# The output projection of a decoder block as seven block products instead of eight

## The chip, the cores and the metric

One core of a Trainium2 chip. The metric is the device time of one execution in microseconds, the median of several runs. Engines are named as the profile does: PE (TensorE, matmul), DVE (VectorE), ACT (ScalarE), POOL (GpSimd) and SP (SyncE, which here only issues transfers). An instruction of one engine runs in the order of that engine's queue. A DMA is issued by an engine, and waits in its queue for whatever its issue waits for.

## The reference

One layer of a decoder trunk over 1024 tokens of width 1024, fp32. The mixers (four HGRN2 heads, four heads of dilated windows, an RWKV-7 group) give 1024 columns, which go through the output projection `w_out` and are added to x. A gated MLP and a gated input embedding follow.

```
z = rmsnorm(h, norm_mix_g) @ w_in
... # o_a: HGRN2 (512 columns), o_b: dilated windows (256), o_c: RWKV-7 (256)
h = h + concatenate([o_a, o_b, o_c]) @ w_out
h = h + conv_glu_ffn(rmsnorm(h, norm_ffn_g), ffn_up, conv_w, conv_b, ffn_down)
gate = sigmoid(rmsnorm(h, norm_ple_g) @ ple_gate)
h = h + gate * (p @ ple_proj)
return rmsnorm(h, final_norm_g)
```

## The kernel before

Everything is held transposed: eight tiles of 128 channels by 1024 tokens, the tokens in two halves of 512 (`HT`). An fp32 product is made of three: each operand is split into a high part (`hi`, a cast on ACT to the type that PE multiplies) and a low part (`lo`, what the cast lost), and high x high, high x low and low x high are summed (`mm3`, L137). Weights are split in `split2` (L110): `hi` by ACT, `lo` either by DVE or POOL as a subtraction, or, where the source in DRAM is passed, as a negation on ACT (L117) and a DMA from POOL's queue that adds the weight on to it (L118). `hi` and `lo` rotate through six buffers each (`WB`), the raw weights through two (`wraw`, L104).

The output projection is `phase_out` (L1239). `rows(m, halves)` takes the weights of one block of 128 output channels, does `dense` over the eight input tiles in the order in which the mixers finish them, and adds the result to `h`, which holds x (eight loads on ACT's queue, L1246); each half row goes to DRAM (`hd`). Row blocks 0 and 1 take both halves at once, then six left halves follow, then six right halves. The mixers' results are split by `o_split` (L1232), `lo` of the right half on POOL.

For the norm of the MLP the squares of `h` are summed into `acc` (`sq_acc`, L213: a square on ACT, an addition on DVE), four matmuls sum over the channels (`rstd`, L188), DVE and POOL make the factor (L191, L195), and four matmuls spread it over a tile (`rstd_spread`, L201). For the left half this happens between the row blocks of the right half; `ffn_norm(0, ...)` then scales and splits the left half of `h` (L1361, L1362, L1369). `pe_load` (L1319) loads two tiles of the per-layer input and two of its projection into two buffers of their own (`praw`), and splits them (`peh`, `pel`); `embed` (L1301) multiplies them after the last row block, and PE fills with its products the time until the right half's factor.

While the RWKV heads run, `project_rest` (L430) goes on with the input projection, and yields after each k-step of six products, so that its work interleaves with that of RWKV. There POOL makes `gnr` (L768), a power on which the group norm of an RWKV head waits, and issues some of the adding DMAs of `split2`. The scheduler of the tile framework sets the order of each queue; `issue_after` places a group of instructions behind another one.

## Time and profile before

| | |
|---|---|
| median of 3 runs | 1404.28 us (1402.86 to 1405.35) |
| the profiled execution | 1403.29 us, span 1401.5 us |
| granted clock of PE | 0.996 |
| PE busy | 1373.6 us, 98% of the span |
| DVE, ACT, POOL busy | 1042.6, 644.2, 361.7 us |

The profile comes from one execution; positions in it are microseconds from the start of its span. The output projection takes about 563 to 643 us of it, the embedding products and the MLP follow. A row of groups has the line, the engine, the operation, what it writes and reads, its shape, and how often; then its busy time, the mean ns of one, and how long the engine stood idle before such instructions, with what ended the idle time. A matmul's duration is longer than its share of the engine's time, since matmuls overlap.

### The profile page before, as it was taken

The numbers are of one execution on the slowest core, as the hardware profiler recorded it, in microseconds if no ns is written. First come the engines' busy times: TensorE is split into PE (matmuls) and PEld (weight loads), VectorE is DVE, ScalarE is ACT, GpSimd is POOL, SyncE is SP. The second block draws the span as 40 slices with busy tenths as digits, with TensorE's granted clock in tenths as the row PEclk, the third lists the DMA queues.
The fourth block names the chain that finished last, engine by engine and source line by source line (L and its number), as shares of the span: only waits on it lengthen the run. The fifth ranks groups of instructions, "written<-read, shape, count | busy, mean of one in ns | idle before, by whom it ended". The sixth has DMA issues, their size and how long they took to land.

```text
span 1401.5 us, 22421 instructions
## 1 busy us (share of the span) xinstructions
PE 1373.6 (98%) x8646; PEld 1114.8 (80%) x8646; DVE 1042.6 (74%) x1614; ACT 644.2 (46%) x1107; POOL 361.7 (26%) x286
## 2 busy tenths in 40 slices
PE   9999999999999999999999999999999999999997
PEld 6878777877878767788788888888888888888886
DVE  7595456835667795458889888888888799778675
ACT  7523323133355584365544343444344444455662
POOL 4210011101222232111345455445453000002231
PEclk9999999999999999999999999999999999999998
DMA  6344322533723322873232322232324963442674
GB/s 231 90 119 101 91 69 68 133 72 88 244 91 106 99 69 89 267 224 130 97 128 98 113 102 88 101 109 98 113 98 163 354 211 113 120 150 62 174 196 149
DMA packets 88475, 182.83 MB, mean 130 GB/s; under 512 B 20912, under 2 KB 23216, under 8 KB 88368
## 3 DMA queue, kind: packets, MB, share of 16 engines
q1 hardware_dynamic: 66784, 147.05, 31.0%
q0 software_dynamic: 9360, 18.88, 7.3%
q10 hardware_dynamic: 12224, 15.47, 3.2%
q8 instruction: 68, 1.11, 0.3%
q14 instruction: 39, 0.32, 0.1%
HBM read 134.96 MB, written 46.40 MB: 129 GB/s over the span
## 4 chain that ended last, share of the span: by engine, by line
PE 83%; issue 7%; DVE 5%; ACT 2%; POOL 2%; DMA 1%; SPq 0%; POOLq 0%; DVEq 0%; ACTq 0%
PE bg L1343 17%; PE bv L1343 13%; PE bv L1644 7%; PE bg L1644 7%; PE dp L142 6%; PE dp L146 6%; PE dp L144 6%; PE swq L1174 1%; PE bv L142 1%; PE bv L146 1%; PE bv L144 1%; PE hsc L1020 1%; PE zp L142 1%; PE bg L142 1%; PE bg L146 1%
## 5 line engine op out<-in xcount | busy, mean ns | idle before, releaser
L142 PE MATMUL dp<-xh,whi 128*128 128x512 f32 x544 | 187.1, 406 | 2.5 <-ACT xh L413 1.2
L144 PE MATMUL dp<-xl,whi 128*128 128x512 f32 x544 | 180.3, 393 | 0.6 <-DVE xl L414 0.5
L146 PE MATMUL dp<-xh,wlo 128*128 128x512 f32 x544 | 179.6, 392 | 0.5 <-DMA wlo<-in_w_out_dram 0.5
L120 POOL TENSOR_TENSOR wlo<-raw,whi 128x512 fp32r<-128x512 f32 x84 | 134.8, 1623 | 75.7 <-ACT whi L114 75.7
L114 ACT CAST whi<-wraw 128x512 fp32r<-128x512 f32 x120 | 72.9, 617 | 153.5 <-PE dp L144 115.4
L1343 PE MATMUL bg<-t,whi 128*128 128x512 f32 x352 | 133.4, 389 | 0.0
L144 PEld LDWEIGHTS dp<-xl,whi 128*128 128x128 f32 x544 | 102.3, 188 | 24.7 <-DVE xl L414 2.6
L146 PEld LDWEIGHTS dp<-xh,wlo 128*128 128x128 f32 x544 | 102.1, 188 | 24.7 <-issue 2.0
L142 PEld LDWEIGHTS dp<-xh,whi 128*128 128x128 f32 x544 | 98.9, 189 | 27.3 <-issue 5.9
L120 POOL TENSOR_TENSOR wlo<-s,whi 128x512 fp32r<-128x512 f32 x44 | 64.6, 1467 | 166.9 <-ACT whi L114 153.7
L1644 PE MATMUL bg<-t,whi 128*128 128x512 f32 x308 | 95.2, 390 | 0.0
L114 ACT CAST whi<-raw 128x512 fp32r<-128x512 f32 x88 | 52.5, 619 | 92.7 <-issue 48.6
L1644 PE MATMUL bv<-t,whi 128*128 128x512 f32 x308 | 94.8, 389 | 0.0
L114 ACT CAST whi<-s 128x512 fp32r<-128x512 f32 x66 | 38.9, 620 | 119.5 <-PE bg L1343 112.8
L1343 PEld LDWEIGHTS bg<-t,whi 128*128 128x128 f32 x352 | 66.0, 188 | 13.7
L118 POOL DMA_DIRECT2D wlo<-in_w_in_dram x28 | 24.8, 898 | 190.0 <-ACT wlo L117 161.6
L195 POOL TENSOR_TENSOR rst<-rst,mhalf 128x4 f32<-128x4 f32 (+1 forms) x9 | 10.1, 1127 | 233.7 <-DVE rst L191 218.0
L1640 ACT CAST t<-t 128x512 fp32r<-128x512 f32 x77 | 47.8, 622 | 45.4 <-PE bv L1644 31.1
L1343 PE MATMUL bg<-t,wlo 128*128 128x512 f32 x176 | 67.5, 389 | 0.0
L1644 PEld LDWEIGHTS bv<-t,whi 128*128 128x128 f32 x308 | 57.8, 188 | 12.0
L1644 PEld LDWEIGHTS bg<-t,whi 128*128 128x128 f32 x308 | 57.8, 188 | 11.9
L120 DVE TENSOR_TENSOR wlo<-wraw,whi 128x512 fp32r<-128x512 f32 x60 | 44.8, 751 | 29.4 <-ACT whi L114 16.5
(423 smaller groups left out, 3464.8 us busy)
## 6 DMA issues: line engine op xcount, KB each, us to landing
raw<-in_ffn_up_dram SPq DMA_DIRECT2D x44, 512.0 KB, 3.3
wraw<-in_w_in_dram SPq DMA_DIRECT2D x28, 512.0 KB, 3.8
z<-zst SPq DMA_DIRECT2D x18, 512.0 KB, 3.2
gb<-ct SPq DMA_DIRECT2D x33, 256.0 KB, 2.1
t<-gb SPq DMA_DIRECT2D x33, 256.0 KB, 2.8
t<-gt SPq DMA_DIRECT2D x33, 256.0 KB, 2.7
zl<-z SPq DMA_DIRECT2D x16, 512.0 KB, 4.6
wraw<-in_ple_gate_dram SPq DMA_DIRECT2D x16, 512.0 KB, 3.8
```

The lines of the kernel that those rows point to most:

```text
L114: self.cast = nc.scalar.copy(hi, src).ins
L118: nc.gpsimd.dma_start(lo, eng, accum_op=ALU.add)
L120: eng.tensor_tensor(lo, src, hi.bitcast(F32), ALU.subtract)
L142: nc.tensor.matmul(ps[hf], wh, xh[hf], start=first, stop=False)
L144: nc.tensor.matmul(ps[hf], wh, xl[hf], start=False, stop=False)
L146: self.step = nc.tensor.matmul(ps[hf], wl, xh[hf], start=False, stop=last).ins
L195: nc.gpsimd.tensor_tensor(r2, r, self.mhalf[:, :n], ALU.pow)
L1020: nc.tensor.matmul(sc[g:g + 64, c, :], ks[:, c * P + g:c * P + g + 64], x, start=True, stop=True)
L1174: m = nc.tensor.matmul(pq[h][:, b:b + w], d["q"][hs, qb * P:nk], d["k"][hs, b:b + w], start=True, stop=True)
L1343: nc.tensor.matmul(ps, w[part == 2][:, s], X[k][part == 1], start=start and k == part == 0, stop=k == 3 and part == 2, skip_group_check=no ...
L1640: nc.scalar.copy(xh, x)
L1644: nc.tensor.matmul(ps[m], wt[part == 2][:, m * P:(m + 1) * P], (xh, xl)[part == 1], start=k == part == 0, stop=k == NK - 1 and part == 2)
```

## The change

The 1024 x 1024 weight is taken as 2 x 2 blocks of 512 (input tiles 6, 7, 0, 1 and 4, 2, 3, 5; output blocks 0 to 3 and 4 to 7), the mixers' result as 2 x 2 blocks of four input tiles by one half of the tokens. Of these, seven block products are made instead of eight, in the order p1, p5, p3, p6, p7, p2, p4, each with four row blocks of 12 products (`job`, `mul`). Four of them need sums of weight blocks, four need sums of the mixers' tiles.

- The weight sums are made while RWKV runs (`out_sums`): in `project_rest`, at k-steps 1, 3 and 6, one step of loading, negating on ACT, adding by DMA from POOL's queue, or storing to DRAM. Over the four row blocks these are 12 negations, 20 adding DMAs, 8 loads and 16 stores, each of 128x512.
- The sums of the mixers' tiles are made where a tile is finished (`o_done`) and between the products (`turn4`, adding DMAs); each operand is split by `pair` on ACT and DVE. What is split first is held in the tiles of an operand that is done.
- The result of p1 is copied to `h` by ACT and that of p5 by DVE (`empty`), and x is added behind each by a DMA from POOL's queue; for the other two quarters x is loaded by SP (`load`). Products that belong to several quarters stay in their PSUM banks and go on being summed there.
- `behind` records an ordering (not a wait) of the instructions issued in it behind a given product: each step of `out_sums` and each of the `extra` steps that `at` puts behind a job.
- `pe_load` takes a buffer of `wraw` instead of `praw`'s own; its four loads come behind jobs 17 to 20. The left half's factor (`factor`) comes behind job 20 (the first row of p2), its spread behind job 21.
- `xpool` is divided, so that part of it is given back later; the columns of `w_out` are put in the order of the tiles on the host.

```diff
+    def behind(self, ins):
+        traced = self.nc.cur_bb.bb.instructions
+        last = traced[-1]
+        yield
+        start = next(k for k in reversed(range(len(traced))) if traced[k] is last) + 1
+        for i in traced[start:]:
+            self.tc.add_manual_dep(i, ins.name, mybir.DependencyInfo(mybir.DependencyClass.NoSync, mybir.DependencyReason.DATA))
...
+        self.sums = self.out_sums()
...
+    def out_sums(self):
+        nc, wo = self.nc, self.a["w_out"]
+        self.S = [{n: self.zpool.tile([P, HT], F32, tag=f"ws{n}{i}", name=f"ws{n}{i}") for n in "1234"} for i in range(4)]
+        for _ in range(15):
+            yield
+        for i in range(4):
+            a11, a12, a21, a22 = (wo[m][:, c] for m in (i, 4 + i) for c in (slice(0, HT), slice(HT, T)))
+            t, u = (self.spool.tile([P, HT], F32, tag="sqt", name=self.nm("wsum"), bufs=2) for _ in (0, 1))
+            def turn(x):
+                nc.scalar.activation(x, x, AF.Copy, scale=-1.0)
+            def add(x, src):
+                nc.gpsimd.dma_start(x, src, accum_op=ALU.add)
+            nc.sync.dma_start(t, a21)
+            nc.sync.dma_start(u, a22)
+            yield
+            turn(t)
+            add(u, a21)
+            yield
+            nc.sync.dma_start(self.S[i]["1"], u)
+            add(t, a11)
+            yield
+            nc.sync.dma_start(self.S[i]["3"], t)
+            turn(u)
+            yield
+            turn(t)
+            add(u, a11)
+            yield
+            add(t, a22)
+            add(u, a12)
+            yield
+            nc.sync.dma_start(self.S[i]["2"], t)
+            nc.sync.dma_start(self.S[i]["4"], u)
...
+                if k in (1, 3, 6):
+                    with self.behind(self.step):
+                        next(self.sums, None)
...
+    def pair(self, dst, src, eng=None):
+        nc = self.nc
+        hi, lo = dst
+        nc.scalar.copy(hi, src)
+        (eng or nc.vector).tensor_tensor(lo, src, hi.bitcast(F32), ALU.subtract)
+    def o_done(self, k):
+        nc = self.nc
+        if self.A is None:
             self.done.append(k)
             return
-        for hf in (0, 1):
-            self.split_x(self.O[k], hf, self.o[k][:, hf * HT:(hf + 1) * HT], alt=hf)
+        o = [self.o[k][:, HT:], self.o[k][:, :HT]]
+        if k in self.FIRST:
+            i = self.FIRST.index(k)
+            t1, t3 = self.Eo[i]
+            nc.vector.tensor_tensor(t1, o[1], o[0], ALU.subtract)
+            self.pair(self.A[i], o[0])
+            self.pair(self.B[i], t1)
+            nc.scalar.activation(t1, t1, AF.Copy, scale=-1.0)
+            nc.scalar.activation(t3, o[1], AF.Copy, scale=-1.0)
+            return
+        i = self.LAST.index(k)
+        for c in (0, 1):
+            if (k, c) not in self.parts:
+                nc.scalar.copy(self.final(k, c, None), o[c])
+        for t in self.Eo[i][::-1]:
+            nc.gpsimd.dma_start(t, self.parts[k, 1], accum_op=ALU.add)
...
+        hold = []
+        def weight(n, i):
+            if not hold:
+                t = self.wpool.tile([P, T], F32, tag="wraw", name=self.nm("wraw"), bufs=2)
+                hold.extend((t[:, left], t[:, right]))
+            t, d = hold.pop(0), src[n](i)
+            nc.sync.dma_start(t, d)
+            return self.split2(t, V if (n, i) in jobs[:16] else d)
...
+        plan = {"p1": (A, "a", 0, 1), "p5": (B, "b", 4, 0), "p3": (D, "b", 0, 0), "p6": (A, "a", 0, 0),
+                "p7": (B, "a", 4, 0), "p2": (C, "c", 0, 1), "p4": (A, "a", 4, 1)}
+        jobs = [(n, i) for n in plan for i in range(4)]
...
+        def sums(m, late):
+            self.sq_acc(acc, self.h[m][:, right if late else left], m == 0)
+        def job(n, i):
+            X, g, row, late = plan[n]
+            if i not in banks[g]:
+                banks[g][i] = self.mxp.tile([P, HT], F32, tag="mx", name=self.nm("zo"))
+            ps, start = banks[g][i], n in ("p1", "p5", "p2")
+            with ExitStack() as order:
+                if self.ends:
+                    order.enter_context(self.tc.issue_after(self.ends[-1]))
+                self.mul((ps, ws.pop((n, i)), X, start))
+            self.ends.append(self.step)
+            if n not in ("p1", "p5"):
+                gather(n, i)
+        def place(n, i):
+            X, g, row, late = plan[n]
+            return self.h[row + i][:, right if late else left], self.a["xT"][row + i][:, right if late else left]
+        def empty(n, i):
+            u, x = place(n, i)
+            if n == "p5":
+                V.tensor_copy(u, banks["b"][i])
+            else:
+                nc.scalar.copy(u, banks["a"][i])
+            nc.gpsimd.dma_start(u, x, accum_op=ALU.add)
+        def load(n, i):
+            nc.sync.dma_start(*place(n, i))
+        def gather(n, i):
+            X, g, row, late = plan[n]
+            m = row + i
+            u = place(n, i)[0]
+            V.tensor_tensor(u, u, banks[g][i], ALU.add)
+            if n in ("p6", "p7", "p2", "p4"):
+                nc.scalar.dma_start(self.hd[m][late], u)
+                if n in ("p6", "p7"):
+                    sums(m, late)
...
+        at(4, [lambda i=i: empty("p5", i) for i in range(4)])
+        at(5, [lambda i=i: (empty("p1", i), load("p3", i)) for i in range(4)])
+        at(16, [lambda i=i: load("p4", i) for i in range(4)])
+        at(3, [lambda i=i: self.pair(D[i], Lo[i][1]) for i in range(4)])
+        at(7, [lambda i=i: self.pair(A[i], Eo[i][0]) for i in range(4)])
+        at(10, [lambda i=i: self.pair(C[i], Lo[i][0]) for i in range(4)])
+        at(11, [lambda i=i: self.pair(B[i], Eo[i][1]) for i in range(4)])
+        at(12, [lambda i=i: turn4(i) for i in range(4)])
+        at(17, [lambda i=i: self.pair(A[i], Lo[i][0]) for i in range(4)])
...
+        at(16, [pools, *(lambda a=a: self.pe_load(*a()) for a in
+                         (lambda: (px, self.pxp, "pT", 0), lambda: (pw, self.pwp, "ple_proj", 0),
+                          lambda: (px, self.pxp, "pT", 1), lambda: (pw, self.pwp, "ple_proj", 1)))])
+        at(20, [factor, norm])
+        at(22, [lambda: [next(self.norm0, None) for _ in (0, 1)] for _ in range(6)])
+        for n, (p, i) in enumerate(jobs):
+            for q in range(0 if n == 0 else n + 4, min(n + 5, len(jobs))):
+                ws[jobs[q]] = weight(*jobs[q])
+            job(p, i)
+            with self.behind(self.ends[-1]):
+                for go in extra.get(n, ()):
+                    go()
...
+        ps, pb = small()
+        with self.behind(self.ends[15]):
+            self.ffn_first()
...
-    def pe_load(self, raws, dst, pool, src, k):
-        raw = raws.tile([P, T], F32, tag="praw", name=self.nm("praw"), bufs=2)
+    def pe_load(self, dst, pool, src, k):
+        raw = self.wpool.tile([P, T], F32, tag="wraw", name=self.nm("praw"), bufs=2)
         self.nc.sync.dma_start(raw, self.a[src][k])
```

Three places where the queues change. First, SP's queue in the second half of the projection. `praw` are the loads of `pe_load`, `wraw` those of the weights (in the change of one half row block each, two to a buffer), `h` the loads of x. Before:

```order
L105 DMA wraw_6300<-in_w_out_dram 128x1024
L105 DMA wraw_6348<-in_w_out_dram 128x1024
L1321 DMA praw_6437<-in_pT_dram 128x1024
L105 DMA wraw_6418<-in_w_out_dram 128x1024
L1321 DMA praw_6445<-in_ple_proj_dram 128x1024
L1321 DMA praw_6497<-in_pT_dram 128x1024
L105 DMA wraw_6478<-in_w_out_dram 128x1024
L1321 DMA praw_6538<-in_ple_proj_dram 128x1024
```

After; `wraw_6518` holds the weights of jobs 24 and 25, the first of p4, `wraw_6585` those of 26 and 27:

```order
L1479 DMA praw_6441<-in_pT_dram 128x1024
L1342 DMA wraw_6449<-in_w_out_dram 128x512
L1381 DMA h_5937<-in_xT_dram 128x512
L1342 DMA wraw_6449<-in_w_out_dram 128x512
L1381 DMA h_5938<-in_xT_dram 128x512
L1479 DMA praw_6476<-in_ple_proj_dram 128x1024
L1479 DMA praw_6510<-in_pT_dram 128x1024
L1342 DMA wraw_6518<-in_w_out_dram 128x512 x2
L1479 DMA praw_6542<-in_ple_proj_dram 128x1024
L1342 DMA wraw_6585<-in_w_out_dram 128x512 x2
```

The `praw` loads stood in buffers of their own; now they and the weights of p4 take turns in the same two, so that a load waits for the splitting of what is two buffers ahead of it.

Second, DVE's queue where the left half's `acc` is finished; `dp`, `zo` are PSUM banks, `rst` the first step of the factor. Before, where `rst_6319` is that of the left half:

```order
L1263 TENSOR_TENSOR h_5848<-h_5848,dp_6193 128x512
L221 TENSOR_TENSOR acc<-acc,sqt_6231 128x512
L1263 TENSOR_TENSOR h_5849<-h_5849,dp_6234 128x512
L120 TENSOR_TENSOR wlo_6309<-wraw_6300,whi_6307 128x512
L221 TENSOR_TENSOR acc<-acc,sqt_6272 128x512
L1325 TENSOR_TENSOR pel_6440<-praw_6437,peh_6439 128x512 x2
L1263 TENSOR_TENSOR h_5844<-h_5844,dp_6275 128x512
L191 TENSOR_SCALAR rst_6319<-ps_ss_6313 128x4
```

After; `h_5931<-h_5931,zo_6525` gathers job 20, and the sum with `sqt_6504` is the last of `acc`:

```order
L1297 TENSOR_TENSOR xl_5383<-xh_5406,xh_5382 128x512
L233 TENSOR_TENSOR acc<-acc,sqt_6435 128x512
L1387 TENSOR_TENSOR h_5937<-h_5937,dp_5973 128x512
L1297 TENSOR_TENSOR xl_5385<-xh_5408,xh_5384 128x512
L1483 TENSOR_TENSOR pel_6444<-praw_6441,peh_6443 128x512 x2
L1387 TENSOR_TENSOR h_5938<-h_5938,dp_5973 128x512
L233 TENSOR_TENSOR acc<-acc,sqt_6470 128x512
L1387 TENSOR_TENSOR h_5931<-h_5931,zo_6525 128x512
L233 TENSOR_TENSOR acc<-acc,sqt_6504 128x512
L1297 TENSOR_TENSOR xl_5387<-xh_5410,xh_5386 128x512
L203 TENSOR_SCALAR rst_6556<-ps_ss_6550 128x4
L1483 TENSOR_TENSOR pel_6479<-praw_6476,peh_6478 128x512 x2
```

The last sum now stands behind the gathering of the job behind which PE's matmul for the factor is queued; on PE, 12 products of job 21 lie between that matmul and the spread. Before, the gathering of the row behind the sums stood between the last sum and `rst` too, but behind the sum.

Third, POOL's queue near the end of the RWKV stage. Before:

```order
L768 TENSOR_TENSOR gnr_1940<-gnv_1937,mhalf 128x8
L698 MEMSET Uc_2524 128x1024
L768 TENSOR_TENSOR gnr_2052<-gnv_2049,mhalf 128x8
L118 DMA wlo_2274<-in_w_in_dram 128x512
L118 DMA wlo_2310<-in_w_in_dram 128x512
```

After:

```order
L821 TENSOR_TENSOR gnr_1973<-gnv_1970,mhalf 128x8
L751 MEMSET Uc_2569 128x1024
L455 DMA wsum_2017<-in_w_out_dram 128x512
L128 DMA wlo_2315<-in_w_in_dram 128x512
L821 TENSOR_TENSOR gnr_2093<-gnv_2090,mhalf 128x8
L128 DMA wlo_2353<-in_w_in_dram 128x512
```

The adding DMA of a `wlo`, which followed the second `gnr`, now stands ahead of it, with one of the weight sums'.

144 lines of the change are left out of this document (71 added, 73 removed).

## The prediction

> **What bounds the kernel now.** I read the page first: the busy shares and the chain that ended last.
>
> ```profile
> PE 1373.6 (98%) x8646; PEld 1114.8 (80%) x8646; DVE 1042.6 (74%) x1614; ACT 644.2 (46%) x1107; POOL 361.7 (26%) x286
> ...
> PE 83%; issue 7%; DVE 5%; ACT 2%; POOL 2%; DMA 1%; SPq 0%; POOLq 0%; DVEq 0%; ACTq 0%
> ```
>
> TensorE has work 98% of the time and stands in 83% of the chain. So a matmul that goes is worth its full cadence, and the question is only what TensorE waits for in its place. The cadence comes from the chain of waits in order of time, around the stage of the output projection (columns: start, length, what).
>
> ```profile
> 577.15 5.36 DMA wlo<-in_w_out_dram
> 582.55 0.50 PE dp L146
> ...
> 666.41 5.44 PE bg L1343 x24
> ```
>
> 24 products of 128x512 take 5.44 us, 0.227 us each (a single one lasts 0.39 us, but they overlap). The first row says that an accumulating transfer's time to landing counts from the start of its issue: issued at 577.15, landed 5.36 us later, and the matmul starts at once. The waits of TensorE between 500 and 690 us, the tail of the mixers and the projection, say what can be had there beside the matmuls:
>
> ```profile
> PE vt L1108 <- DVE ho L1102: 3.0, 2, 1.8
> ...
> PE dp L146 <- DMA wlo<-in_w_out_dram: 0.5, 1, 0.5
> ...
> PE dp L142 <- DVE h L1263: 0.4, 1, 0.4
> ```
>
> The projection itself (563 to 660 us) waits 0.9 us in all. The other engines, by stretches of 40 us (PE, PEld, DVE, ACT, POOL, then clock, DMA share, GB/s):
>
> ```profile
> 560.00:600.00 40.00, 38.96 (x172) 31.31 (x173) 16.14 (x24) 15.05 (x26) 6.50 (x7) 1.00 0.84 258
> 600.00:640.00 40.00, 40.00 (x184) 33.23 (x183) 28.27 (x46) 24.34 (x44) 5.43 (x6) 1.00 0.67 190
> 640.00:680.00 40.00, 40.00 (x184) 33.13 (x183) 35.15 (x55) 23.77 (x37) 5.55 (x5) 1.00 0.41 158
> ```
>
> VectorE is 40% busy where the projection begins, 71% in its second half, 88% behind it. What the change adds lands on an engine that has room early and none late.
>
> **What goes.** Before, 8 row blocks x 2 halves x 8 k x 3 parts = 384 products; after, 7 block products x 4 rows x 4 k x 3 parts = 336. 48 x 0.227 = **10.9 us**. The two waits of the projection (0.5 and 0.4) hang on tiles that no longer exist in that form: **0.9 us**, taken as gone. Together -11.8.
>
> **What comes.** The prices of the small operations, from the groups of 563 to 690 us (count, busy, mean ns, idle before):
>
> ```profile
> L1263 DVE TENSOR_TENSOR h<-h,dp 128x512 f32<-128x512 f32 x16 | 10.8, 684 | 22.4 <-PE dp L146 22.4
> L221 DVE TENSOR_TENSOR acc<-acc,sqt 128x512 f32<-128x512 f32 x14 | 9.6, 687 | 2.5 <-ACT sqt L220 2.3
> ...
> L120 DVE TENSOR_TENSOR wlo<-wraw,whi 128x512 fp32r<-128x512 f32 x11 | 7.6, 689 | 5.9 <-PE dp L144 4.3 <-ACT whi L114 1.6
> L117 ACT ACTIVATE wlo<-whi 128x512 fp32r<-128x512 f32 x11 | 6.9, 631 | 4.5 <-DVE h L1263 4.2
> ...
> L1325 DVE TENSOR_TENSOR pel<-praw,peh 128x512 fp32r<-128x512 f32 x8 | 5.2, 687 | 3.7 <-ACT peh L1324 3.7
> ...
> L1324 ACT CAST peh<-praw 128x512 fp32r<-128x512 f32 x8 | 4.6, 616 | 4.2 <-DMA praw<-in_ple_proj_dram 4.0 <-DMA praw<-in_pT_dram 0.3
> ```
>
> A VectorE operation on 128x512 takes 0.69 us, a ScalarE one 0.62, and in a queue they follow each other somewhat closer, since the next begins before the last one's end:
>
> ```profile
> 640.28 1.29 DVE L120 TENSOR_TENSOR wlo<-raw,whi 128x512 fp32r<-128x512 f32 x2
> ```
>
> Two take 1.29 us, so each further one costs 0.6. The transfers, from the issues between 565 and 660 us, and their spread (min/median/max) from the views by tile and by line:
>
> ```profile
> hd<-h ACTq DMA_DIRECT2D x16, 256.0 KB, 3.2
> wlo<-in_w_out_dram POOLq DMA_DIRECT2D x11, 256.0 KB, 5.4
> ...
> praw<-in_ple_proj_dram SPq DMA_DIRECT2D x2, 512.0 KB, 5.5
> ```
>
> ```profile
> L118 POOL DMA_DIRECT2D wlo<-in_w_out_dram x11: 857/858/927, 577.1 to 629.0; - x11
> ...
> DMA to landing us min/median/max: 3.8/5.4/7.5
> ```
>
> ```profile
> L1321 SPq DMA_DIRECT2D praw<-in_ple_proj_dram x2: 328/620/911, 611.2 to 620.5; - x2
> ...
> DMA to landing us min/median/max: 3.7/6.0/7.3
> ```
>
> ```profile
> L1264 ACTq DMA_DIRECT2D hd<-h x16: 326/327/390, 569.5 to 644.0; - x16
> ...
> DMA to landing us min/median/max: 2.0/3.2/8.2
> ```
>
> I number the 28 row blocks (jobs) 0 to 27 in their order; each is 12 products, 2.72 us. Five places cost TensorE something.
>
> (a) The factor of the left half. Its matmul `ps_ss` is queued on TensorE right behind block 20, and its input is the last `acc` sum. On VectorE that sum stands behind the gathering of block 20 itself (the second pair of listings of the change). So it waits at least for one gathering and one sum, 0.7 + 0.6 = 1.3 us. The longer way goes along the queues from the end of block 18: the half's copy and the gathering of 18 (1.3), ScalarE's `hd` issue 0.33 and two `peh` casts (to 2.9), two `pel` on VectorE (4.2), the gathering of 19 behind them (4.8), `hd`, a negation and a square on ScalarE (0.33 + 0.63 + 0.63, and a cast in between: 6.8), the sum (7.4). Block 20 ends at 5.4. Wait 2.0; I take **2.0**, since every row of it is in the queue whatever the load. Before, the 24 products of the next half row lay between the last row of the left half and `ps_ss`, and nothing waited.
>
> (b) The weights of the last product. `pe_load` no longer has buffers of its own but shares the two of `wraw` with the weights. In SP's queue (first pair of listings) the load of `praw_6476` waits for the `pel` of the one before, and the weights of blocks 24 and 25 (`wraw_6518`) wait for the `pel` of `praw_6476`. Again from the end of block 18: first `pel` done 4.2; load 5.5, so 9.7; casts 1.2 and `pel` 1.3, so 12.2; weights 256 KB, 3.2 as `hd`, so 15.4; two casts and the negation 1.8, so 17.2; accumulating transfer 5.4, so 22.6. TensorE gets to block 24 after blocks 19 to 23 (13.6), the wait of (a) (2.0) and the eight small matmuls of the factor (0.9), and wants `wlo` two products later: 17.0. The ends of queues run into each other by some 0.2, so I take **5.4**. Bounds by the extremes of the rows above: with 3.7, 2.0 and 3.8 it is 4.6 less, 0.8; with 7.3, 7.5 and, for the 256 KB, 5.1 (some way to its rare 8.2) it is 5.8 more, 11.2. The medians are taken since at that point one write, one weight load and one accumulating transfer run per block, the same mix as in the rows.
>
> [...]
>
> (c) The factor of the right half. Before:
>
> ```profile
> 643.24 0.69 DVE L1263 TENSOR_TENSOR h<-h,dp 128x512 f32<-128x512 f32 x1 [0.47 <-PE dp L146]
> ...
> 646.05 0.68 DVE L221 TENSOR_TENSOR acc<-acc,sqt 128x512 f32<-128x512 f32 x1
> ```
>
> ```profile
> 647.12 0.94 PE L188 MATMUL ps_ss<-few,acc 128*128 128x1 f32 x8
> ...
> 649.42 0.65 PE L201 MATMUL ps_ss<-cst,rst 128*128 128x128 f32 x4
> ```
>
> ```profile
> 648.35 1.02 POOL L195 TENSOR_TENSOR rst<-rst,mhalf 128x4 f32<-128x4 f32 x1 [2.77 <-DVE rst L191]
> ```
>
> The last sum came 3.5 us behind the last gathering, and six matmuls covered the power on POOL. After, VectorE reaches the last gathering some 2 us late (the left half's eight scalings and eight residues, 16 x 0.6, fall between blocks 21 and 27) and has nine rows behind it until the last sum, 9 x 0.6: 8 us behind the last product. TensorE has 28 embedding products to fill, 28 x 0.227 = 6.4: wait 1.6. The spread now follows two matmuls behind the sum instead of six: 0.9. **2.5**; nothing at the least, if (b) gives VectorE the time to catch up.
>
> (d) In the RWKV stage POOL's order turns round (third pair of listings).
>
> ```profile
> 196.54 1.64 POOL L768 TENSOR_TENSOR gnr<-gnv,mhalf 128x8 f32<-128x8 f32 x1 [15.86 <-DVE gnv L766]
> 198.12 0.92 POOL L118 DMA_DIRECT2D wlo<-in_w_in_dram  x1
> ```
>
> ```profile
> 196.42 0.63 ACT L117 ACTIVATE wlo<-whi 128x512 fp32r<-128x512 f32 x1
> ```
>
> ```profile
> 199.05 0.63 PE L775 MATMUL yt<-cst,y 128*128 128x128 f32 x4 [0.60 <-DVE y L769]
> ```
>
> Now the DMA issue stands first: its negation ends at 197.05, the issue takes 0.92, so `gnr` begins at 197.97 instead of 196.54. TensorE already waits 0.60 for its result: **1.4** more.
>
> (e) The weight sums: twelve negations of 0.63 on ScalarE, twenty accumulating issues on POOL, 24 transfers on SP, all in `project_rest`. ScalarE is 46% busy and TensorE's waits for it are few, so I take 0. With no cover at all they cost 12 x 0.63 = 7.6.
>
> (f) One `wlo` of the projection's weights (0.69) stands on VectorE between the reduction and the scaling of the last HGRN head, on which `vt` waits already (3.0 in the row above): **0.5**, between 0 and 0.7.
>
> The p1 and p5 copies, the loads of x, the pairs of operands (28 on VectorE against 8, with the 16 residues that POOL had) lie in blocks 4 to 16, where VectorE was 40% busy: 0.
>
> **Sum**: -10.9 - 0.9 + 2.0 + 5.4 + 2.5 + 1.4 + 0.5 = 0.0. The profiled execution (1403.29 us, span 1401.5) would stay at 1403.3; the median of the runs lies 1.0 above it (1404.28), so **1404.3**. About 0.2% (2.8 us) is what a measurement of this kernel can tell from no change.
>
> **Rivals.** *The matmuls' gain stays* (36%): the transfers of (b) land near their short ends and VectorE keeps up. (a) 1.3, (b) 0.8, (c) 0.9 (the spread alone), (d) 1.4, (f) nothing: net -7.4, 1396.9. For it: DMA share falls to 0.41 behind 640 us, and the shortest 256 KB took 2.0. Against: the loads of `praw` took 6.0 in the middle though the share was 0.67. With (c) and (d) at nothing too it is -9.7, 1394.6.
>
> *The shared buffers decide* (22%), on the other side: in (b) three transfers in series land at their long ends. Wait 11.2, the rest as above, net +5.8, 1410.1. It makes the kernel slower by over 2.8 once (b) exceeds 8.2, that is, when the three land 2.8 later in sum than I took them. For it: x, weights and `hd` run at once in 560 to 600 us at a share of 0.84, and the loads of x now stretch to block 18. Against: in SP's queue the last of them stands before `praw_6476`, so the chain itself runs without them.
>
> *The sums' turns stall RWKV* (4%): (e) at half of its bound, 3.8, 1408.1. Against: a load and the turn that uses it are two or three steps of six products apart, 2.7 to 4.1 us, and the turn follows ScalarE's own work of that step.
>
> *The products aren't saved*, since TensorE is idle in their place anyway: ruled out by the 98%, except by (a) to (c), which are counted.
>
> **Chances and range.** Forecast 38%; faster 36%, slower 26% (the 22 and the 4). The range reaches from the fast case's far end to just over the slow one: 1395 to 1411; the forecast's own is 1401.5 to 1407.
>
> **What would show it.** Right: 48 fewer matmuls in the projection; TensorE waiting for `ps_ss` <- `acc` about 2 us twice; a wait of 4 to 7 us for a DMA of `wlo` at block 24; `yt` <- `y` at 2.0. Wrong: block 24 starting without a wait over 2 us (then the time is near 1399), or a wait of over 8; waits in blocks 0 to 15, of which I expect none; a longer RWKV stage by more than 2 us.

## The result, and the profile after

The changed kernel takes 1427.24 us (median of 4 runs, 1422.01 to 1429.45) against 1403.74 us before (4 runs, 1402.86 to 1405.35): a ratio of 1.0161, 95% interval 1.0129 to 1.0193. It is 23.5 us slower. The prediction was 1404.3, with a range to 1411; both the forecast and the range were wrong. The profiled execution took 1429.45 us, span 1427.7.

The page, busy time of each engine:

```profile
PE 1376.9 (96%) x8598; PEld 1114.9 (78%) x8598; DVE 1062.1 (74%) x1652; ACT 663.1 (46%) x1143; POOL 382.5 (27%) x312
```

There are 48 matmuls fewer (8598 against 8646), and yet PE is busy 3.3 us longer. It also stands idle longer: 1427.7 - 1376.9 = 50.8 us against 1401.5 - 1373.6 = 27.9. The waits of PE over the whole span, longest in total first (total, times, longest):

```profile
PE dp L1501 <- DVE h L1387: 6.9, 6, 2.8
PE dp L1501 <- DMA wlo<-in_w_out_dram: 4.7, 1, 4.7
PE py L848 <- DMA Tc<-Tz: 4.5, 2, 4.0
PE vt L1161 <- DVE ho L1155: 3.5, 2, 1.8
...
PE ps_ss L200 <- DVE acc L233: 2.2, 2, 1.4
...
PE yt L828 <- DVE y L822: 1.9, 1, 1.9
...
PE sk L848 <- DVE MG L944: 1.4, 1, 1.4
...
PE ps_ss L213 <- POOL rst L207: 0.8, 1, 0.8
```

`wlo`, `acc`, `y` and `rst` are the waits (a) to (d) of the prediction, at about the predicted size. The first row, the row for `Tc` and the row for `MG` were not in it. What the busy time hides is in the granted clock. The view by stretches, cut where the waits for `Tc`, for `h`, for `wlo`, and for the second `acc` lie and behind them (PE, PEld, DVE, ACT, POOL, clock, DMA share, GB/s; a transfer counts whole in the stretch in which it starts, so a DMA share can pass 1):

```profile
290.00:298.00 8.00, 4.12 (x19) 3.08 (x17) 1.03 (x2) 0.60 (x1) 1.67 (x2) 1.00 1.13 177
298.00:306.00 8.00, 7.39 (x96) 5.94 (x98) 0.37 (x1) 3.81 (x7) 0.08 (x1) 0.57 0.86 183
598.00:602.00 4.00, 1.22 (x6) 0.71 (x5) 3.83 (x7) 3.49 (x8) 1.53 (x2) 1.00 0.73 189
602.00:606.00 4.00, 4.00 (x13) 3.10 (x12) 1.29 (x3) 2.54 (x5) 0.87 (x1) 0.58 0.97 235
639.00:644.00 5.00, 0.94 (x5) 0.44 (x3) 2.66 (x5) 2.42 (x5) 0.91 (x2) 0.96 0.98 206
644.00:654.00 10.00, 8.47 (x20) 6.19 (x21) 5.64 (x9) 5.60 (x11) 1.73 (x2) 0.51 0.54 129
666.00:671.00 5.00, 3.71 (x18) 2.25 (x17) 3.35 (x7) 2.57 (x4) 0.43 (x1) 0.99 0.58 208
671.00:678.00 7.00, 6.34 (x18) 5.14 (x19) 5.19 (x8) 1.01 (x1) 0.61 (x1) 0.52 0.32 125
```

In each pair the first row holds the wait, at full clock or nearly so, and the second the work behind it at about half: 10 us with 20 matmuls instead of 44. In the record of the granted clock these stretches are 6.8, 3.4, 10.2, 6.8 us long, and a fifth of 3.4 lies at 715 us: 30.7 us at half speed, worth 15.4 us. The kernel before has none between 14 and 1392 us.

So the 26.2 us between the two spans are: -10.9 for the matmuls, +22.9 of idle time, +15.4 of half clock, in sum 27.4, about a microsecond from what was measured. Half clock that falls into a wait costs nothing there; the stretch of 10.2 us begins 1.1 us before the wait for `wlo` ends.

By place: in the stage behind RWKV the `hsc` product that waits 0.6 us for `qt` in both kernels starts at 460.17 against 449.44 us, 10.7 late. The last wait of the HGRN tail ends 11.6 late, and the MLP's first product behind a wait for `bv` starts at 713.86 against 689.60, 24.3 late. RWKV lost 11, the projection lost 13 where 11 were to be gained, and the half clock at 715 the rest.

### The profile page after: what moved, and what is told of

Read it like the earlier page. It is cut to its first block, busy times and chain, and to the rows that moved or that the text cites. A ratio compares the mean times of both kernels' runs of the same rounds, so it can differ in the third digit from the quotient of the medians.

```text
span 1427.7 us, 22537 instructions
## 1 busy us (share of the span) xinstructions
PE 1376.9 (96%) x8598; PEld 1114.9 (78%) x8598; DVE 1062.1 (74%) x1652; ACT 663.1 (46%) x1143; POOL 382.5 (27%) x312
## 4 chain that ended last, share of the span: by engine, by line
PE 51%; POOL 0%; DVE 0%; issue 0%; DMA 0%; POOLq 0%; ACT 0%; DVEq 0%
PE bg L1501 16%; PE bv L1501 12%; PE bv L1803 7%; PE bg L1803 7%; PE bv L152 1%; PE bv L154 1%; PE bv L156 1%; PE bg L152 1%; PE bg L156 1%; PE bg L154 1%; DMA raw<-in_ffn_up_dram 0%; PE dp L154 0%; PE dp L152 0%; PE dp L156 0%; POOL h L1892 0%
## 5 line engine op out<-in xcount | busy, mean ns | idle before, releaser
L152 PE MATMUL dp<-xh,whi 128*128 128x512 f32 x416 | 139.6, 411 | 2.8 <-ACT xh L424 2.0
L154 PE MATMUL dp<-xl,whi 128*128 128x512 f32 x416 | 132.9, 394 | 0.9 <-DVE xl L425 0.9
L156 PE MATMUL dp<-xh,wlo 128*128 128x512 f32 x416 | 132.4, 393 | 0.0
L154 PEld LDWEIGHTS dp<-xl,whi 128*128 128x128 f32 x416 | 78.8, 189 | 18.8 <-DVE xl L425 1.8
L156 PEld LDWEIGHTS dp<-xh,wlo 128*128 128x128 f32 x416 | 78.4, 189 | 18.9 <-issue 1.5
L152 PEld LDWEIGHTS dp<-xh,whi 128*128 128x128 f32 x416 | 75.2, 190 | 22.9 <-issue 5.6
L1501 PEld LDWEIGHTS bg<-t,whi 128*128 128x128 f32 x352 | 66.0, 188 | 13.7
L207 POOL TENSOR_TENSOR rst<-rst,mhalf 128x4 f32<-128x4 f32 (+1 forms) x9 | 10.2, 1134 | 239.6 <-DVE rst L203 223.8
L1800 DVE TENSOR_TENSOR t<-t,t 128x512 fp32r<-128x512 f32 x77 | 54.9, 713 | 8.0 <-ACT t L1799 7.8
```

The costliest lines, as they stand in the source:

```text
L152: nc.tensor.matmul(ps[hf], wh, xh[hf], start=first, stop=False)
L154: nc.tensor.matmul(ps[hf], wh, xl[hf], start=False, stop=False)
L156: self.step = nc.tensor.matmul(ps[hf], wl, xh[hf], start=False, stop=last).ins
L207: nc.gpsimd.tensor_tensor(r2, r, self.mhalf[:, :n], ALU.pow)
L1501: self.step = nc.tensor.matmul(ps, w[part == 2][:, s], X[k][part == 1], start=start and k == part == 0, stop=k == 3 and part == 2, skip_gr ...
L1800: V.tensor_tensor(xl, x, xh.bitcast(F32), ALU.subtract)
```

## The experiments

Three questions stood open. Why does the product wait for `h`, which the prediction's walk along the queues did not show? What made the transfers so slow? And what does the clock do? The changed kernel's four runs reach from 1422.0 to 1429.5 us, so gains of about 5 us in a median are to be read with care, and the waits in the traces carry more of the argument. For the second question, the transfers issued between 575 and 640 us, by queue (packets, MB, share of the 16 DMA engines' time) and by tile (count, KB, median us to landing), in the changed kernel:

```profile
q1 hardware_dynamic: 4483, 10.27, 47.9%
q0 software_dynamic: 2592, 4.72, 41.5%
q10 hardware_dynamic: 1437, 2.62, 10.8%
...
hd<-h ACTq DMA_DIRECT2D x10, 256.0 KB, 6.0
...
h<-in_xT_dram SPq DMA_DIRECT2D x8, 256.0 KB, 7.4
h<-in_xT_dram POOLq DMA_DIRECT2D x8, 256.0 KB, 8.9
```

and the queues of the kernel before in the same stretch:

```profile
q1 hardware_dynamic: 1872, 6.82, 33.0%
q0 software_dynamic: 1584, 2.88, 26.4%
q10 hardware_dynamic: 1984, 3.63, 15.0%
```

The shares add up to 74% before and to 100% after. A 256 KB write of `hd` takes 6.0 us where it took 3.1. POOL's queue, which carries the adding transfers, holds the engines for 41.5% x 65 us / 4.72 MB = 5.7 us per MB; SP's plain loads for 3.0. An adding transfer cost about twice a plain one here. It did so before the change too: 6.0 against 3.1 us per MB (26.4% for 2.88 MB, 33.0% for 6.82).

The first and longest wait for `h`, 2.8 us at 601.32, shows how the first two questions hang together. On DVE, just before it (in brackets the idle time before, and what ended it):

```profile
594.17 0.69 DVE L1387 TENSOR_TENSOR h<-h,zo 128x512 f32<-128x512 f32 x1 [1.11 <-DMA h<-in_xT_dram]
...
598.17 0.69 DVE L1387 TENSOR_TENSOR h<-h,zo 128x512 f32<-128x512 f32 x1 [2.11 <-PE dp L1501]
```

The loads of x that these two additions need landed at 594.08 and 598.08, 11.2 and 10.8 us after their issue. For the second the view names PE, but the addition starts 0.09 us behind the landing, as the first one does. Three more operations stood before the addition for which PE waited (the gathering of block 12, at 600.58).

### Row blocks paired otherwise

p1, p6, p7 and p4 sum into four banks of PSUM, laid two by two into two tiles of the program; consecutive row blocks shared a tile. The product of block 13 therefore waited for the gathering of block 12 (DVE's addition of its bank to `h`), though it writes another half.

```diff
-        banks = {"a": {i: g1[i // 2][:, (left, right)[i % 2]] for i in range(4)}, "b": {}, "c": {}}
+        banks = {"a": {i: g1[i % 2][:, (left, right)[i // 2]] for i in range(4)}, "b": {}, "c": {}}
```

> The row blocks of the sum that p1, p6, p7 and p4 share are laid into two PSUM tiles the other way: blocks 0 and 2 in one, 1 and 3 in the other (before 0 and 1, 2 and 3). Nothing else changes. Theory (a product waits for the gathering of its neighbour because the two share a PSUM tile): TensorE's six waits for h (6.9 us, line of the gathering) fall under 1 us in all, the half clock behind the first of them (3.4 us, worth 1.7) goes, time about 1427 - 6 - 1.7 = 1419. Rival (VectorE is simply late with the gatherings): the waits move one block on, to blocks 14, 18, 26, and the time stays within 2 us of 1427.

Measured: 1421.47 us, ratio to before 1.0124 (1.0109 to 1.0139), so 5.8 us better than the change. The six waits for `h` are gone. But the waits of PE between 570 and 720 us now begin with one that is longer than all six:

```profile
PE ps_ss L200 <- DVE acc L233: 8.2, 1, 8.2
PE dp L1501 <- DMA wlo<-in_w_out_dram: 1.8, 1, 1.8
```

What ACT did before it (start, length, what; in brackets the idle time before, and what ended it):

```profile
623.29 1.14 ACT L1482 CAST peh<-praw 128x512 fp32r<-128x512 f32 x2 [8.55 <-DMA praw<-in_pT_dram]
```

The first `praw` load was issued at 615.88 and landed 7.4 us later; ACT's queue stood still on it, `pel` on DVE behind ACT, the gathering and the sum behind `pel`. That is the chain of (a) as the prediction walked it, with another transfer in it. The shared tile was a cause of waits, as the theory said; it was not what bounded the stage. Neither theory had a transfer in it.

### The embedding's loads behind the weights of p4

```diff
-        at(16, [pools, *(lambda a=a: self.pe_load(*a()) for a in
+        at(16, [pools])
+        at(22, [lambda a=a: self.pe_load(*a()) for a in
```

> The four loads of pe_load are placed behind jobs 22 to 25 instead of 17 to 20, so that in SP's queue and in the two buffers all weights of p4 stand before them. Theory (chain through the two shared buffers, and a half clock behind its wait): the wait of 4.7 us for wlo at block 24 goes, with it the half clock of 10.2 us (5.1): about 1427 - 4.7 - 5.1 = 1417. Rival one (the wait alone costs, the clock drops for another reason): 1422.5. Rival two (the embedding's operands come too late instead): a wait of over 3 us at the first embedding product, and no gain.

Measured: 1422.89 us, 1.0137 (1.0122 to 1.0152), 4.4 us better. The wait for `wlo` is gone, which confirms the chain through the two shared buffers, but the six waits for `h` grew:

```profile
PE dp L1502 <- DVE h L1387: 16.3, 6, 5.6
```

Two of them are 5.6 and 5.4 us long, and behind each lies a stretch of 6.8 us at half clock. The gain of the half clock that was expected did not come, because another wait took the place.

### Without the weight sums

Left out are the sums' loads, negations, adding transfers and stores; the four products that use them take plain blocks of the weight, so that the projection is not computed.

```diff
-        for i in range(4):
+        for i in range(0):
...
-               **{f"p{p}": lambda i, n=n: self.S[i][n] for p, n in ("51", "62", "73", "34")}}
+               **{f"p{p}": lambda i: wo[4 + i][:, left] for p in (5, 6, 7, 3)}}
```

> Leaves out the weight sums in the RWKV stage (all their loads, negations, adding transfers and stores); the four products that want a sum take a plain block of the weight from DRAM instead, of the same size, so the output is not the projection. Theory (their transfers delay RWKV's own): the waits for Tc (4.5), for y (1.9, of which 0.6 was there before) and for MG (1.4) go, with the half clock of 6.8 us behind Tc (3.4): about 1427 - 4.5 - 1.3 - 1.4 - 3.4 = 1416.6. Rival (the sums cost ScalarE's and POOL's time, not transfers): Tc still waits over 3 us. Rival (the order of the queues, which shifts anyway, made these waits): the time stays within 3 us of 1427.

Measured: 1416.42 us, 1.0084 (1.0064 to 1.0103), 10.8 us better, as the theory said. The waits of PE between 100 and 480 us hold none for `Tc` or `MG` any more, and 0.6 for `y`.

In the changed kernel, between 270 and 300 us, where RWKV takes its inverse through DRAM (`Tz`, `Tc`), the same loads landed late among the sums' transfers:

```profile
wsum<-in_w_out_dram POOLq DMA_DIRECT2D x5, 256.0 KB, 5.3
...
Tz<-Tb SPq DMA_DIRECT2D x1, 256.0 KB, 5.4
...
Tc<-Tz SPq DMA_DIRECT2D x4, 64.0 KB, 6.6
```

Before, `Tz` took 2.9 us and `Tc` 3.6. ScalarE's time, which the prediction weighed for the sums, had no part in the largest of these waits.

### Three edits together, and a pause of the sums

The blocks paired otherwise, the embedding's loads behind the weights of p4, and eight k-steps of pause before the third weight sum (`for _ in range(8 * (i == 2)): yield`).

> The first two edits together, and the third weight sum begins eight k-steps later, so that its transfers don't stand in the stretch in which RWKV transposes its inverse through DRAM (Tz, Tc). The full computation. If waits and half clock add up as in the three theories: 1427 - 7.7 - 9.8 - 7.9 (Tc and its half clock) = about 1402, level with the kernel before or 1 to 2 us faster. If the clock drops wherever many small waits come together, the remaining waits (acc and rst 3.0, y 1.9, MG 1.4) keep a half clock or two: 1405 to 1408.

Measured: 1422.8 us, 1.0129 (1.0103 to 1.0155). The gains did not add up. `Tc` fell to 0.8 us, but other waits grew or came new:

```profile
PE dp L1504 <- DVE h L1389: 8.0, 3, 4.2
...
PE hsc L1075 <- DVE qt L1088: 3.4, 3, 2.6
...
PE sk L850 <- DVE MG L946: 2.7, 1, 2.7
```

The last transfer of the sums now lands at 392.6 us instead of 336.7, and the wait of 2.6 at an `hsc` ends at 404.9, where HGRN starts. That the later sums made it is likely, but not shown. The wait for `MG` ends at 152.1, ahead of the pause, and has nothing to do with it.

### Low parts on POOL instead of adding transfers

```diff
-            return self.split2(t, V if (n, i) in jobs[:16] else d)
+            return self.split2(t, V if (n, i) in jobs[:16] else G)
```

> The low parts of the weights of p7, p2 and p4 are subtracted on POOL (as the MLP's weights are, 1.5 us each) instead of by a negation on ACT and an adding transfer. Nothing else changes. Theory (the 16 DMA engines are full in the projection): between 575 and 640 us POOL's queue moved 4.7 MB in 41.5% of the engines' time, 5.7 us per MB; twelve transfers less are 3.1 MB, 18 us of about 95 that the stage asks for. The DMA share falls from 1.0 to about 0.8, the loads of x and weights land in 4 to 5 us instead of 6.6 to 7.4, the wait at block 24 falls from 4.7 to under 2 and its half clock (10.2) goes: about 1427 - 4 - 5 - 2 = 1416. Rival (the queues of DVE and ACT are simply behind): the share falls but the waits stay, time within 3 us of 1427. Rival (POOL's subtractions come later than the transfers did): waits for wlo from POOL, no gain.

Measured: 1422.44 us, 1.0138 (1.0113 to 1.0164). The DMA share between 600 and 640 us falls to 0.6 to 0.8, and the wait for `wlo` is gone, as expected. The pairs' waits stay, and the weights' place is taken by a wait for an operand of the MLP (`t`):

```profile
PE dp L1501 <- DVE h L1387: 8.5, 5, 4.2
PE dp L1501 <- ACT t L1519: 3.3, 1, 3.3
```

5 us of the 11 expected came, with runs from 1419.6 to 1427.0. That the full DMA engines were one cause fits; the edit also takes twelve negations off ACT, and the two were not separated. It has a price of its own: between 560 and 690 us nine of VectorE's operations on two tiles of 128x512 (`TENSOR_TENSOR`), each beside an operation of POOL, took 1.1 to 1.8 us, in sum 6.7 us more than at 0.69, the longest that any took without POOL beside it.

### x up front, without copies

p1 and p5 are added to x by DVE like the other products; x is loaded whole from ACT's queue, as before the change. This takes back the part of the change that copies two products and adds x behind them.

> x is loaded into h whole and up front from ACT's queue, as in the kernel before, and p1 and p5 are added to it by DVE like the other products: no copies, no adding transfer of x, no loads of x between the products. Nothing else changes. Theory (DMA engines full): eight adding transfers (2.1 MB, 12 us of the engines) and eight loads (6 us) leave the stretch from 578 to 622 us, and the loads fall where the share is 0.1 to 0.6; the first wait for a gathering (2.8) falls to about 0.8 and its half clock goes, the landings fall to 5 us: about 1427 - 2 - 1.7 - 2 = 1421. Rival (the four additions more on DVE delay it further): the waits for h grow, 1429 or more.

Measured: 1428.95 us, 1.0182 (1.0167 to 1.0198), no better than the change. The rival is nearer in time, but the reason is another one. A wait of 6.3 us has come at the last HGRN head:

```profile
567.88 1.94 PE L1161 MATMUL vt<-cst,ho 128*128 128x128 f32 x8 [6.33 <-DVE ho L1155]
571.26 0.80 PE L1499 MATMUL dp<-xh,whi 128*128 128x512 f32 x1 [1.44 <-DVE h L1388]
```

The head's own chain (its last `hpo`, the norm, `ho`, `vt`) is no longer than in the changed kernel: 6.3 us from 561.55 here, 6.8 from 564.80 there. But there 21 products of the projection lie in it, and here none. Only block 0 was done before it. Block 1 shares its tile, and now waits for the gathering of block 0, which is the first addition to x and stands behind `ho` in DVE's queue, at 570.52; x's loads stand behind that head's square in ACT's queue, and the first is issued at 564.54. So the copies with x added behind do what they are for: the first products don't wait for x.

### The edits against transfers together

Paired row blocks, low parts on POOL, x up front, and the MLP's first weights behind the last product (`self.behind(self.ends[27])` instead of `ends[15]`).

> Four edits together: the row blocks paired 0, 2 and 1, 3 in PSUM; the low parts of p7, p2, p4 on POOL; x loaded up front and added by DVE; the MLP's first weights behind the last product instead of behind block 15. The full computation. Theory (the DMA engines set the projection's pace, and each long wait adds a half clock): the stage asks for 95 - 18 - 18 - 6 = 53 us of transfers in 76 us, share about 0.7; all waits of the projection beyond 1 to 2 us go and with them its half clock (20.5 us, worth 10.2): what is left is -10.9 in the projection and about +11 in the RWKV stage, so 1404 to 1408. Rival (queues of DVE): the wait for acc stays at 5 to 8 us as in the run with the blocks paired alone, over 1413.

Measured: 1422.95 us, 1.0137 (1.012 to 1.0154). The transfers are no longer the bound:

```profile
600.00:620.00 20.00, 18.57 (x82) 15.07 (x81) 19.07 (x23) 9.62 (x18) 8.46 (x6) 1.00 0.38 131
```

The DMA share is 0.38, and DVE is busy 19.07 of 20 us. 5.6 us of that are the edit's own doing: six of its operations took 1.2 to 1.8 us instead of 0.69, each beside a subtraction on POOL. The time did not follow. The wait on `ho` is 5.9 us again, since only two blocks could be made before x was there (24 products, against 42 in the changed kernel). And a wait of 3.7 us on `e` has come in the MLP, where ACT's copy stands behind casts that wait for VectorE; the MLP's first weights had landed 36 us before it, so that they came too late isn't shown.

### The sums on POOL from three tiles

The same, with the weight sums made by POOL from three tiles in SBUF, without negations and adding transfers (16 loads, 16 operations, 16 stores).

> As the run before, and the weight sums are made with three tiles by POOL in SBUF: 16 plain loads, 16 additions or subtractions of 1.5 us on POOL and 16 stores, no negations and no adding transfers. The full computation. Theory (adding transfers cost the engines twice a plain one's time and crowd out RWKV's own): the stage's transfers for the sums fall from about 30 + 6 + 11 = 47 us of engine time to 13 + 11 = 24; the waits for Tc fall from 4.5 to under 2 without a half clock, y keeps its wait only if POOL's order still puts an issue ahead of gnr: 6 to 8 us less than the run before, 1397 to 1401. Rival (any transfer there delays Tc): as the run before within 2 us.

Measured: 1422.8 us, 1.0143 (1.0127 to 1.0159), as the run before. The waits for `Tc` fell from 5.4 to 3.5 and `y` to 0.6, but `MG` waits 2.3: ACT stood still for 5.2 us on a load of the input projection's weights, which was issued 1.5 us behind the first of the sums' loads and landed after 8.2 us (4.1 before the change). There the rival was right. For `Tc` it was not: `Tz` landed in 2.9 us and the `Tc` in 2.6 to 3.3, no later than before the change, so it was the adding transfers that had delayed them. What is left of that wait comes from VectorE, which has to finish `Tb` before `Tz` can be issued (290.17 us here, 285.17 in the changed kernel). Two of its operations, and what POOL did then:

```profile
280.39 1.33 DVE L731 TENSOR_TENSOR Tb<-Tb,Tt 64x192 f32<-64x192 f32 x1
285.33 2.08 DVE L731 TENSOR_TENSOR Tb<-Tb,Tt 64x156 f32<-64x156 f32 x1
```

```profile
280.02 1.49 POOL L456 TENSOR_TENSOR wsum<-wsum,wsum 128x512 f32<-128x512 f32 x1 [5.01 <-DMA wsum<-in_w_out_dram]
285.63 1.59 POOL L462 TENSOR_TENSOR wsum<-wsum,wsum 128x512 f32<-128x512 f32 x1
```

In the changed kernel the same two take 0.35 and 0.31 us. Four such operations, each beside a sum on POOL, took 4.7 us more in all, nearly the 5.0 by which `Tz` is late. So the sums moved from the DMA engines to POOL delayed RWKV by another way, which neither theory named.

### Waits put into the kernel before

Four waits in the MLP's up projection, where PE otherwise has none: a chain of n + 1 small ACT operations, a small matmul that adds zero, and the products held behind it.

```diff
+            n = {5: 3, 8: 7, 11: 12, 14: 20}.get(f, 0)
+            if n:
+                tok = self.tok.tile([P, 8], F32, tag="tok", name=self.nm("tok"), bufs=1)
+                with self.tc.issue_after(self.last):
+                    nc.scalar.activation(tok, d["G"][:, HT:HT + 8], AF.Copy, scale=0.0)
+                    for _ in range(n):
+                        nc.scalar.activation(tok, tok, AF.Copy, scale=1.0)
+                    self.last = nc.tensor.matmul(d["V"][:, :8], self.ident, tok, start=False, stop=False, skip_group_check=True).ins
```

> The kernel before, with four waits put into the MLP's up projection, 70 us and more apart, where TensorE never waits: behind the products p5 and p2 of units 5, 8, 11 and 14 a chain of 4, 8, 13 and 21 small copies on ACT starts from their result, and one more small matmul that adds zero waits for its end; the products behind it are held behind it. Theory (a wait of TensorE costs its length and, from some length on, a stretch at half clock): waits of about 1.5, 2.5, 4 and 6 us; behind the two longest, perhaps the second, the granted clock is 0.5 for 3.4 us or a multiple; the span grows by the sum of the waits and half of these stretches, so by 14 and 5 to 10 more. Rival (the half clock in the changed kernel has another cause, such as small matmuls or the load on the DMA engines): the clock stays at 1.0 and the span grows by the waits alone.

Measured: 1443.56 us, 1.0279 (1.0257 to 1.0302), span 1441.4. The waits are 2.2, 3.1, 4.3 and 6.3 us:

```profile
PE bv L1528 <- ACT tok L1527: 15.9, 4, 6.3
```

The view by stretches, each holding the 8 us behind one of them:

```profile
778.20:786.00 7.80, 7.80 (x28) 6.28 (x29) 3.27 (x4) 0.62 (x1) 2.73 (x2) 0.78 0.24 86
...
841.00:849.00 8.00, 7.74 (x22) 6.17 (x23) 3.93 (x5) 0.82 (x2) 1.99 (x2) 0.57 0.43 164
...
906.90:915.00 8.10, 8.04 (x25) 6.43 (x26) 1.15 (x2) 0.63 (x2) 1.29 (x1) 0.64 0.08 32
...
974.00:982.00 8.00, 7.79 (x28) 6.41 (x29) 0.82 (x2) 0.77 (x2) 1.29 (x1) 0.78 0.24 82
```

Behind the 2.2 us the clock is at half for 3.4 us, behind each of the others for 6.8, of which a part falls into the longer waits. The load on the DMA engines is low here (0.08 to 0.43), and full-size products stand on both sides, with only the one small matmul between them. So waits do it, and the rival falls. Of the 39.9 us that the span grew, 15.9 are the waits and 13.7 the half clock (27.3 us, 3.4 of them behind a wait of 2.4 at 510 us). The remaining 10 lie in the cadence. Outside these stretches the full-size products of this kernel follow each other every 0.230 us from 640 us on and every 0.233 us from 1110 on, where the kernel before has 0.227 throughout; over the 2680 of them between 640 and 1300 us that is 10.8 us. It begins ahead of the first wait put in, at 776 us, so the waits don't make it. Why it is so is open; neither theory has it.

### Paired row blocks and low parts on POOL

> The full computation with two edits: the row blocks paired 0, 2 and 1, 3 in PSUM, and the low parts of p7, p2, p4 on POOL. Alone, the first moved its waits into one of 8.2 us for acc, with ACT waiting 8.5 us for a load; the second took the wait for wlo away but kept those of the pairs. Theory (the shared tiles and the full DMA engines are two causes, and each hides behind the other): together the waits for h fall under 1 us each, acc under 2.5, none for wlo; the projection's half clock falls from 20.5 us to at most 7: 1427 - 6.9 - 4.7 - 6.8 + 1.5 = about 1410. Rival (DVE's work itself is the bound): acc waits over 5 us, 1418 or more.

Measured: 1419.03 us, 1.0106 (1.008 to 1.0132), the lowest median of the full computations (its runs reach from 1416.6 to 1422.9, those with the blocks paired alone from 1419.5 to 1422.8), but still 15 us slower than before. The waits of PE between 570 and 720 us:

```profile
PE dp L1501 <- DVE h L1387: 3.4, 2, 2.2
PE bv L1501 <- DVE bv L1674: 2.8, 1, 2.8
PE vt L1161 <- DVE ho L1155: 1.8, 1, 1.8
PE ps_ss L200 <- DVE acc L233: 1.7, 1, 1.7
```

`acc` fell from 8.2 to 1.7 and `wlo` is gone: the shared tiles and the full engines were two causes that hid each other. The projection's own half clock fell to 6.8 us, and 3.4 lie at 702. That the time is 9 us above the 1410 expected is partly RWKV: in this execution `Tc` waited 5.5 us, with 10.2 us of half clock behind.

### The same without the sums

As above, and the sums left out, so that the projection is not computed.

> The two edits of the run before, and the weight sums left out (four products take plain blocks of the weight, so the output is not the projection). It shows what the seven products are worth when the sums cost nothing. Theory (the RWKV stage loses 11 us to the sums, apart from the projection's own loss): 11 us less than the run before, about 1399, that is 4 to 5 us below the kernel before. Rival (without the sums the projection loses more, since waits move): within 4 us of the run before.

Measured: 1407.41 us (10 runs), 1.0019 (1.0008 to 1.0031): 11.6 us less than with the sums, as the theory said of RWKV, but not below the kernel before, where the theory had about 1399. Even here the projection gives back what its 48 matmuls save. The view by stretches of 20 us in it:

```profile
595.00:615.00 20.00, 19.25 (x78) 15.48 (x77) 19.43 (x27) 10.11 (x19) 6.90 (x5) 0.92 0.90 294
```

DVE is busy 19.43 of 20 us and the DMA share is still 0.90. Of DVE's time 3.6 us are four operations that took 1.2 to 1.8 us beside POOL's subtractions. PE's idle time over the whole span is 36.4 us, 8.5 more than before, and 6.8 us run at half clock: -10.9 + 8.5 + 3.4 = +1.0, against 1.6 measured in the span. The profiled execution, 1404.92 us, is the fastest of the ten. What would take DVE's load off was not tried, nor a run that relieves the DMA engines without the work on POOL; so how much of this last loss is DVE's own work, and how much POOL's beside it, is open.

## Why the prediction was wrong, point by point

Three steps failed: the line that puts the copies, the loads of x and the pairs of operands at 0, the term (e) at 0, and the price of a wait, which left the clock out. In the terms of the span: -11.8 for what goes, 9.6 for the five terms that were counted, 6.9 for the waits for `h`, 5.9 for `Tc` and `MG`, and 15.4 for the clock give 26.0, against 26.2 measured.

- **What goes**, -10.9: right, 48 matmuls at an unchanged 0.227 us. The two old waits (0.9) are gone too.
- **(a)** 2.0, with a least value of 1.3: measured 1.38. **(b)** 5.4: measured 4.72, at block 24, and gone when the loads were moved. **(c)** 2.5: measured 0.85 + 0.80. **(d)** 1.4: measured 1.3 more on `yt`. **(f)** 0.5: measured 0.5 more on `vt` (3.5 against 3.0). Together these are 9.6 where 11.8 were written. (b), (c) and (d) were right in place and mechanism. In (a) it was the least value that held: DVE waited for the last product of block 20 (at 628.32), and one gathering and one sum followed; the long way from block 18, by which 2.0 was written, didn't bind. (f) was luck: the `wlo` did stand where it was expected, but the wait at the last head stayed as it was (1.80, then 1.79), and the 0.5 came at the head before it (1.22, then 1.73).
- **The line "the p1 and p5 copies, the loads of x, the pairs of operands ... 0"** failed, and with it "waits in blocks 0 to 15, of which I expect none". It took room on DVE from its busy share before and asked nothing of the DMA engines. The first wait for `h` (2.8 us at 601) comes with DVE behind, and DVE is behind since it stood still 1.1 and 2.1 us for loads of x that took 11 us to land. And a wait of each product for its neighbour's gathering was missed, because the four sums share two PSUM tiles: 6.9 us in six waits. That DVE's own work would have been too much is not shown: it is busy 19 of 20 us only in runs that also move subtractions to POOL, and there 3.6 to 5.6 us of it are operations that took longer beside POOL.
- **The medians of the transfers in (b), "the same mix as in the rows"**, did not hold: the load, the weights and the adding transfer of that chain landed after 4.2, 3.8 and 6.5 us instead of 5.5, 3.2 and 5.4. That (b) came out near is partly luck, since these errors nearly cancel. The step that was missing is a sum of the transfers' demand. From the rows of before: SP's queue 33.0% of 65 us for 6.82 MB, 3.1 us per MB; ACT's 2.7; POOL's 6.0. The changed stage asks for 13.6 MB on SP (43 us), 4.2 on ACT (11), 5.2 of adding transfers of weights and x (31), 2.1 of adding transfers of operands (13): by this estimate 85 to 98 us of all 16 engines, for 76 us of products. The kernel before asks for about 68 in 87. This was to be had from the profile of the kernel before.
- **(e)**, the sums at 0 with a cover of ScalarE's idle time: wrong by 11 us, as both pairs of runs with and without the sums show (10.8 and 11.6, of which (d) had 1.3). The bound of 7.6 was on the wrong resource: `Tc` waited for transfers that landed late among the adding ones, `MG` for a load that was issued behind the sums' loads and took 7.2 us instead of 4.1, and only `y` (1.3) for POOL's order, which (d) had.
- **The clock** was no term at all. The prediction priced every wait at its length; the five stretches at half clock cost 15.4 us, more than half of the slowdown. The profile of before had no such stretch in its middle, and its longest wait was 2.4 us; the forecast itself contained one of 5.4.
- **The rivals.** "The shared buffers decide" gave 1410 on the right side, but by long landings in (b), which did not come. "The sums' turns stall RWKV" got 4% and has 11 us of the loss, by another way than it named. The sum of 0.0 came from terms mostly of the right kind, with three missing.

## What to carry to other kernels

When a change saves work on an engine that is never idle, add up what its stage then asks of each other resource, the DMA engines first, with an adding transfer counted twice (1.9 times a plain load's time per byte here); where one asks for longer than the engine's new time, the gain is in doubt. Here the transfers asked for an estimated 85 to 98 us beside 76 us of products, and the gain did not come. Price a wait of TensorE of about 3 us or more at its length and some 1.5 to 4.6 us more for the clock, which is half of what the half clock lasted behind such waits here (all 25 waits of 2.9 us or more had a stretch of it); a shorter wait brought it sometimes (22 of the 142 between 0.8 and 2.9 us). Look which tiles, not which elements, two consecutive steps share: six waits of 6.9 us in all went here when the rows were paired otherwise. And when work moves from the DMA engines to POOL, look what VectorE's operations take beside it: here up to 1.8 us on 128x512, where 0.69 was the longest without POOL.

## What the runs showed of the hardware

- Half clock came in stretches of 3.4, 6.8, 10.2 and 13.7 us, behind waits of PE or beginning in them. In the profiles of all these kernels there are 25 waits of 2.9 us or more between the start and the last 30 us, and each was followed or overlapped by such a stretch; of 14 waits between 2.1 and 2.9 us, 8 were, and of 128 between 0.8 and 2.1 us, 14. So the length of a wait alone doesn't decide: 13 of the 46 stretches there have no wait of 2.1 us or more in the 7 us before them, two of these in the changed kernel (behind 0.85 and 0.80 us, and behind 1.76) and both in the last run. The same wait of 2.4 us for `hV` at 510 us ran on at full clock in the kernel before and was followed by half clock in the run with the four waits:

```profile
510.00:514.00 4.00, 3.90 (x47) 3.21 (x48) 4.00 (x9) 3.97 (x7) 1.61 (x2) 1.00 0.53 174
```

```profile
510.00:514.00 4.00, 4.00 (x41) 3.52 (x39) 3.35 (x9) 3.97 (x7) 0.92 (x1) 0.59 0.56 139
```

- Between 575 and 640 us the adding transfers, all on POOL's queue, held the 16 DMA engines 1.9 times as long per byte as SP's plain loads: 5.7 against 3.0 us per MB after the change, 6.0 against 3.1 before.
- Some of VectorE's operations took longer beside POOL's. In the run with low parts on POOL, 88 operations of VectorE on two tiles of 128x512 between 560 and 690 us with no operation of POOL beside them took at most 0.69 us; of 24 that had one beside them, nine took 1.1 to 1.8. In RWKV, in the run with the sums on POOL, operations that take 0.31 to 0.41 us in the changed kernel took 1.3 to 2.1 while POOL made a sum.
